# Gated attention's values turned through DRAM and VectorE instead of on TensorE

## The chip, the cores and the metric

The kernel runs on one core of a Trainium2 chip. The metric is the time of one execution on the device in microseconds (us); of the kernel before there are three runs, and their median counts.

The engines of the core work side by side, each through its own queue in order: TensorE (PE; PEld is its weight load), VectorE (DVE), ScalarE (ACT), GpSimd (POOL) and SyncE (SP). They wait for each other by semaphores. Matmuls write to PSUM, which has banks; the other data lie in SBUF, and weights and inputs in DRAM.

## What is computed

The reference is one block of a decoder: an RMS norm, one wide projection, two kinds of attention side by side (a forgetting attention with 8 heads and a gated linear attention with 4), their gated sum, an output projection, and a squared-ReLU MLP. There are 256 tokens and 16 learned meta tokens, 272 in all, and a model width of 2048. Cut to the gated attention:

```python
GLA_HEADS, GLA_DK, GLA_DV, GLA_CHUNK = 4, 256, 512, 64
def gated_linear_attention(q, k, v, g):
    # S_t = diag(alpha_t) S_{t-1} + k_t^T v_t,  o_t = q_t S_t, chunked
    ...
    q_dec, k_inv = qc * jnp.exp(b), kc * jnp.exp(-b)
    a = jnp.where(causal, einsum(q_dec, k_inv), 0.0)
    o_intra = einsum(a, vc)
    ...
o_gla = gated_linear_attention(gq, gk, gv, g_log)
o_gla = head_rmsnorm(o_gla, gla_norm_g) * silu(gr)
```

All is in float32.

## The kernel before

**Tiling.** Activations lie transposed: 128 features on the partitions, tokens along a row. Every projection is a gemm of one weight chunk (2048 x 128) with 16 steps of 128 features. To reach float32 accuracy, numbers are split in a high and a low part, and a step takes two matmuls (`gemm2`, lines 144 and 145, 512 and 256 columns) or three (`gemm_all`, lines 161 to 163, 272 columns). A weight chunk comes in two halves: SyncE's DMA fills `raw`, ScalarE casts the high part (line 128), VectorE subtracts it to get the low part (line 129), and the pair lies in one of five `wt` buffers. Gemm results come to one of three PSUM banks (pool `pg`); all other PSUM tiles share five (pool `px`).

**A head of gated attention** (`gla_head`) takes two key gemms, two query gemms, four value gemms (called V0 to V3 here) and four gate gemms. Each value gemm yields 128 of the head's 512 value columns, transposed: columns on the partitions, tokens along the row. Its eviction on VectorE scales it into `vT` (256 tokens, line 563) and `vE` (the last 16, line 564). The attention needs the values with tokens on the partitions, so `turn` transposes them: TensorE makes eight 128x128 transposes (lines 553 and 554) and one of 64x128 (line 555) as matmuls with the identity; ScalarE and VectorE split the first part to `v0`, and ScalarE copies the others to `v1` and `v2`.

`scores` multiplies queries and keys into the bank `pa` (line 535). ScalarE copies it (lines 536 and 537), GpSimd masks it with `affine_select` (line 542), and ScalarE and VectorE split it into `a0h` and `a0l` (lines 177 and 178). `outputs` multiplies scores and values into two `po` banks, copies them to `oT` and squares them to `so`. `sums` adds the squares over the partitions and takes the inverse root on VectorE (`root`, lines 206 to 212, whose room is `so`). `scale` multiplies `oT` by the norm's gain `ggn` and that factor (line 596), then by the gate `sg` (line 598), and splits the result to `og`.

**The order of the work.** `later(n, fn)` puts `fn` aside, and it runs when `n` further gemms have been issued; so `scores`, `turn`, `outputs`, `sums` and `scale` of one head are laid between the gemms of that head and the next. On each engine a list scheduler then fixes a queue. The attention's tiles lie in the pool `att` with one buffer for a tag, and `vT` and `so` have the same tag: the next head's values may only be written when the factor in `so` has been used.

Of the kernel before, what the change touches and what calls it, by code (L numbers as in the profile page):

```python
# [7 lines left out]
F32 = mybir.dt.float32  # L8
# [4 lines left out]
ALU = mybir.AluOpType  # L13
# [3 lines left out]
P = 128  # L17
D = 2048
KT = D // P
NM = 16  # L20
NT = 256
NA = NM + NT
EPS = 1e-6
FOX_H, FOX_D = 8, 128
GLA_H, GLA_DK, GLA_DV = 4, 256, 512
# [8 lines left out]
BIG = 3.0e38  # L34
RAW = 5
NL = 4

O_FQ, O_FK, O_FV, O_FF = 0, 1024, 2048, 3072
O_GQ, O_GK, O_GV, O_GR = 3080, 4104, 5128, 7176
# [29 lines left out]
def trunk(ctx: ExitStack, tc: tile.TileContext, hT, w_small, w_all, consts, w_alpha2, out):  # L69
    nc = tc.nc  # L70
    serial = [0]

    def nm(s):
        serial[0] += 1
        return f"{s}_{serial[0]}"
# [5 lines left out]
    dram = ctx.enter_context(tc.tile_pool(name="dram", bufs=1, space=bass.MemoryType.DRAM))  # L81
    pg = ctx.enter_context(tc.tile_pool(name="pg", bufs=3, space=PSUM))
    px = ctx.enter_context(tc.tile_pool(name="px", bufs=5, space=PSUM))
# [3 lines left out]
    def bank(pool, s):  # L87
        return pool.tile([P, 512], F32, tag="bank", name=nm(s))
# [5 lines left out]
    def later(n, fn):  # L94
        waiting.append([n, fn])
# [60 lines left out]
    def gemm_all(w, x, n=NA):  # L156
# [7 lines left out]
        issued()  # L164
        return ps

    def total(ps, t=None):

        b = tmp.tile([P, NT], F32, tag="evb", name=nm("evb"))
        nc.scalar.copy(b, ps[:, NT:512])  # L170
        if t is None:
            t = tmp.tile([P, NT], F32, tag="evt", name=nm("evt"), bufs=4)
        nc.vector.tensor_tensor(t, ps[:, 0:NT], b, op=ALU.add)  # L173
        return t

    def split_to(dst_hi, dst_lo, src):
        nc.scalar.copy(dst_hi, src)
        nc.vector.tensor_tensor(dst_lo, src, dst_hi.bitcast(F32), op=ALU.subtract)

    def split(pool, tag, src, bufs=None):  # L180

        kw = {} if bufs is None else {"bufs": bufs}
        hi = pool.tile(list(src.shape), F32R, tag=tag + "h", name=nm(tag + "h"), **kw)
        lo = pool.tile(list(src.shape), F32R, tag=tag + "l", name=nm(tag + "l"), **kw)
        split_to(hi, lo, src)
        return hi, lo
# [66 lines left out]
    ident, scan = cons[:, 0:P], cons[:, P : P + NA]  # L253
    ggn, ba, bf = cons[:, 400:416], cons[:, 416:424], cons[:, 424:425]
# [252 lines left out]
    def gla_head(hd, sg, ready=None):  # L507

        ki = att.tile([P, 2, NA], F32, tag="ki", name=nm("ki"))
        q0 = ready[0] if ready else att.tile([P, 2, NT], F32, tag="qd", name=nm("qd"))  # L510
        q1 = att.tile([P, 2, NT - G1], F32, tag="q1", name=nm("q1"))
        q2 = att.tile([P, 2, NM], F32, tag="q2", name=nm("q2"))
        k2 = att.tile([P, 2, 4, NM], F32, tag="k2", name=nm("k2"))
        for i in range(2):
            ps = ready[1] if ready and i == 0 else gemm_all(next_weights(), x)
            nc.vector.tensor_tensor(ki[:, i, :], ps[:, 0:NA], rb, op=ALU.mult)
        for i in range(2):
            t = q0[:, i, :] if ready else total(gemm2(next_weights(), xt))
            nc.vector.scalar_tensor_tensor(q0[:, i, :], t, GLA_DK ** -0.5, rbt, op0=ALU.mult, op1=ALU.mult)
        e = decay[hd]  # L520
        nc.vector.tensor_tensor(ki, ki, e[:, :, Q:], op=ALU.mult)
        nc.vector.tensor_copy(k2, ki[:, :, 2 * P :].unsqueeze(2).to_broadcast([P, 2, 4, NM]))
        nc.vector.tensor_tensor(q1, q0[:, :, G1:], e[:, :, NT : Q - NM], op=ALU.mult)
        nc.vector.tensor_tensor(q2, q0[:, :, G2:], e[:, :, Q - NM : Q], op=ALU.mult)
        nc.vector.tensor_tensor(q0, q0, e[:, :, 0:NT], op=ALU.mult)

        at1 = att.tile([P, NT - G1], F32, tag="at1", name=nm("at1"))

        def scores():
            pa = bank(px, "pa")  # L530
            p0, p1, p2 = pa[:, 0:NT], pa[:, NT : 2 * NT - G1], pa[0 : 4 * NM, 2 * NT - G1 : Q]
            for dst, k, q in ((p0, ki[:, :, 0:P], q0), (p1, ki[:, :, P : 2 * P], q1),
                              (p2, k2.rearrange("p a j s -> p a (j s)"), q2)):
                for a in range(2):
                    nc.tensor.matmul(dst, k[:, a, :], q[:, a, :], start=(a == 0), stop=(a == 1))  # L535
            nc.scalar.copy(at0, p0)
            nc.scalar.copy(at1, p1)
            nc.vector.tensor_tensor(at2[0 : 4 * NM].rearrange("p (j q) -> p j q", q=NM),
                                    p2.unsqueeze(1).to_broadcast([4 * NM, 4, NM]),
                                    diag[0 : 4 * NM].rearrange("p (j q) -> p j q", q=NM), op=ALU.mult)  # L540
            for ap, n, base in ((at0[:, 0:G1], G1, NM), (at1[:, 0:P], P, 0)):
                nc.gpsimd.affine_select(ap, ap, pattern=[[1, n]], compare_op=ALU.is_ge, fill=0.0, base=base,
                                        channel_multiplier=-1)

        v1 = att.tile([P, GLA_DV], F32, tag="v1", name=nm("v1"))
        vT = att.tile([P, 4, 2 * P], F32, tag="vT", name=nm("vT"))
        vE = att.tile([P, 4 * NM], F32, tag="vE", name=nm("vE"))

        def turn():
            pv = [bank(px, n) for n in ("p0", "p1", "p2")]  # L550
            for i in range(4):
                cols = slice(P * i, P * (i + 1))
                nc.tensor.transpose(pv[0][:, cols], vT[:, i, 0:P], ident)  # L553
                nc.tensor.transpose(pv[1][:, cols], vT[:, i, P : 2 * P], ident)
            nc.tensor.transpose(pv[2][0 : 4 * NM, 0:P], vE, ident)
            split_to(*v0, pv[0])
            nc.scalar.copy(v1, pv[1])
            nc.scalar.copy(v2[0 : 4 * NM], pv[2][0 : 4 * NM, 0:P])

        later(5, scores)  # L560
        for i in range(4):
            ps = gemm_all(next_weights(), x)
            nc.vector.tensor_tensor(vT[:, i, :], ps[:, 0 : 2 * P], rb[:, 0 : 2 * P], op=ALU.mult)
            nc.vector.tensor_tensor(vE[:, NM * i : NM * (i + 1)], ps[:, 2 * P : NA], rb[:, 2 * P :], op=ALU.mult)
        later(1, turn)

        oT = att.tile([P, 4, NT], F32, tag="oT", name=nm("oT"))
        st = {}

        def outputs():  # L570
            a0 = split(att, "a0", at0)
            so = st["so"] = att.tile([P, 4, NT], F32, tag="vT", name=nm("so"))
            po = [bank(px, "po").rearrange("p (j t) -> p j t", t=NT) for _ in range(2)]
            for c in range(4):
                three(po[c // 2][:, c % 2, :], [e[:, P * c : P * (c + 1)] for e in v0], a0, c % 2 == 0, False)
            for i, pj in enumerate(po):
                for j in range(2):
                    v = slice(P * (2 * i + j), P * (2 * i + j + 1))
                    nc.tensor.matmul(pj[:, j, G1:], v1[:, v], at1, start=False, stop=False)  # L579
                nc.tensor.matmul(pj[:, :, G2:], v2, at2[:, 2 * NM * i : 2 * NM * (i + 1)], start=False, stop=True)  # L580
                nc.scalar.copy(oT[:, 2 * i : 2 * i + 2, :], pj)
                nc.scalar.activation(so[:, 2 * i : 2 * i + 2, :], pj, AF.Square)
            nc.gpsimd.tensor_tensor(so[:, 0:2, :], so[:, 0:2, :], so[:, 2:4, :], op=ALU.add)
            nc.gpsimd.tensor_tensor(so[:, 0, :], so[:, 0, :], so[:, 1, :], op=ALU.add)
            st["sq"] = split(att, "sq", so[:, 0, :])

        def sums():
            pr = bank(px, "pr")[:, 0:NT]
            for i in range(2):
                nc.tensor.matmul(pr, ones_r, st["sq"][i], start=(i == 0), stop=(i == 1))  # L590
            st["y"] = root(pr, NT, 1.0 / GLA_DV, [st["so"][:, i, :] for i in (1, 2, 3, 3)])

        def scale():
            for i in range(4):
                j = 4 * hd + i
                nc.vector.scalar_tensor_tensor(oT[:, i, :], oT[:, i, :], ggn[:, j : j + 1], st["y"], op0=ALU.mult,
                                               op1=ALU.mult)
                nc.vector.tensor_tensor(oT[:, i, :], oT[:, i, :], st["sg"][:, i, :], op=ALU.mult)
                split_to(og_tile()[j][:, 0, :], og_tile()[j][:, 1, :], oT[:, i, :])

        later(2, outputs)
        later(3, sums)
        if sg is None:
            sg = gla_gates(None)
            st["sg"] = sg
            scale()
        else:
            st["sg"] = sg
            later(8, scale)

    att = cum.enter_context(tc.tile_pool(name="att", bufs=1, reuse_waits="tile"))

# [386 lines left out]
```

## Time and profile before

| | |
|---|---|
| median of 3 runs | 1596.85 us (1596.45 to 1598.58) |
| the profiled execution | 1599.16 us, of which the span is 1597.5 us |
| PE busy | 1587.4 us (99% of the span) |
| PEld busy | 1439.0 us (90%) |
| DVE busy | 1056.2 us (66%) |
| ACT busy | 780.0 us (49%) |
| POOL busy | 90.4 us (6%) |

The span runs from the first to the last recorded instruction; the execution's own time lies 1.7 us over it. A busy share is that of an engine's recorded instructions in the span. In a timeline each row has the start, the duration, the engine, the line of the kernel and what it writes and reads; "x4" says that four like instructions are drawn together. Durations of matmuls overlap, so the distance between two starts is what one takes of TensorE's time.

### The profile page before, as it was taken

What the parts mean: (1) busy time and instruction counts of PE and PEld (TensorE: products, weight loads), DVE (VectorE), ACT (ScalarE), POOL (GpSimd) and SP (SyncE); (2) the same over time, 40 slices, a digit from 0 to 9 for tenths busy, and PEclk for the clock granted to TensorE, in tenths of its full rate; (3) what the DMA queues carried; (4) which work ended last, traced back from release to release, by engine and by line L of the source; (5) the groups of instructions that cost most, each with busy time, mean ns of one, the idle gap of its engine ahead of it and who ended that gap; (6) DMA issues with size and microseconds to landing.
All of it is one profiled execution on the core that took longest, in us unless ns stands there. A gap on an engine that the chain in (4) does not pass through costs nothing.

```text
span 1597.5 us, 25251 instructions
## 1 busy us (share of the span) xinstructions
PE 1587.4 (99%) x9838; PEld 1439.0 (90%) x9838; DVE 1056.2 (66%) x1616; ACT 780.0 (49%) x1174; POOL 90.4 (6%) x139
## 2 busy tenths in 40 slices
PE   9999999999999999999999999999999999999998
PEld 8999999999998888888888888888888888888887
DVE  7777757575556656656677776667655776567665
ACT  6676444454445444444554443344433444344553
POOL 0000000010100000000012000000000000000011
PEclk9999999999999999999999999999999999999999
DMA  9444545455445555555565555555555555555552
GB/s 309 170 144 168 179 154 182 159 186 166 166 159 175 193 188 193 188 186 193 178 204 189 185 187 195 187 192 188 185 197 186 193 188 190 193 186 193 188 183 95
DMA packets 89464, 293.15 MB, mean 184 GB/s; under 512 B 9392, under 2 KB 19520, under 8 KB 89344
## 3 DMA queue, kind: packets, MB, share of 16 engines
q1 hardware_dynamic: 88176, 289.67, 54.0%
q0 software_dynamic: 448, 1.13, 0.3%
q8 instruction: 77, 1.26, 0.3%
q10 hardware_dynamic: 720, 0.74, 0.2%
q14 instruction: 43, 0.35, 0.1%
HBM read 289.39 MB, written 2.11 MB: 182 GB/s over the span
## 4 chain that ended last, share of the span: by engine, by line
PE 99%; DVE 0%; DMA 0%; ACT 0%; issue 0%; DVEq 0%; ACTq 0%
PE ps L144 50%; PE ps L145 27%; PE psa L162 5%; PE psa L161 5%; PE psa L163 5%; PE ps L359 1%; PE ps L892 1%; PE ps L366 1%; PE ps L879 0%; PE pa L535 0%; PE po L579 0%; PE psa L621 0%; DMA h<-hT_dram 0%; DVE scaled L924 0%; PE pq L691 0%; PE p L553 0%
## 5 line engine op out<-in xcount | busy, mean ns | idle before, releaser
L129 DVE TENSOR_TENSOR wt<-raw,wt 128x1024 fp32r<-128x1024 f32 x522 | 644.1, 1234 | 349.6 <-ACT wt L128 343.9
L128 ACT CAST wt<-raw 128x1024 fp32r<-128x1024 f32 x522 | 548.7, 1052 | 511.0 <-PE ps L145 277.5
L144 PE MATMUL ps<-x,wt 128*128 128x512 f32 x1952 | 679.8, 391 | 0.0
L145 PE MATMUL ps<-x,wt 128*128 128x256 f32 x1952 | 550.6, 282 | 0.0
L144 PEld LDWEIGHTS ps<-x,wt 128*128 128x128 f32 x1952 | 366.4, 188 | 75.8
L145 PEld LDWEIGHTS ps<-x,wt 128*128 128x128 f32 x1952 | 368.9, 189 | 0.2
L144 PE MATMUL ps<-a,wt 128*128 128x512 f32 x960 | 333.0, 390 | 0.0
L145 PE MATMUL ps<-a,wt 128*128 128x256 f32 x960 | 270.7, 282 | 0.0
L144 PEld LDWEIGHTS ps<-a,wt 128*128 128x128 f32 x960 | 180.1, 188 | 37.8
L145 PEld LDWEIGHTS ps<-a,wt 128*128 128x128 f32 x960 | 181.4, 189 | 0.0
L161 PE MATMUL psa<-x,wt 128*128 128x272 f32 x624 | 180.8, 290 | 0.0
L163 PE MATMUL psa<-x,wt 128*128 128x272 f32 x624 | 180.6, 289 | 0.0
L162 PE MATMUL psa<-x,wt 128*128 128x272 f32 x624 | 180.2, 289 | 0.0
L170 ACT COPY evb<-ps 128x256 f32<-128x256 f32 x160 | 59.4, 373 | 231.2 <-PE ps L145 229.3
L173 DVE TENSOR_TENSOR evt<-ps,evb 128x256 f32<-128x256 f32 x158 | 67.0, 425 | 100.0 <-ACT evb L170 99.8
L161 PEld LDWEIGHTS psa<-x,wt 128*128 128x128 f32 x624 | 117.2, 188 | 0.7
L162 PEld LDWEIGHTS psa<-x,wt 128*128 128x128 f32 x624 | 117.3, 188 | 0.0
L163 PEld LDWEIGHTS psa<-x,wt 128*128 128x128 f32 x624 | 117.2, 188 | 0.0
L144 PE MATMUL ps<-og,wt 128*128 128x512 f32 x256 | 89.2, 390 | 0.0
L144 PE MATMUL ps<-y,wt 128*128 128x512 f32 x256 | 88.8, 390 | 0.0
L802 POOL TENSOR_TENSOR acc<-acc,hsq 128x256 f32<-128x256 f32 x26 | 29.0, 1115 | 767.3 <-ACT hsq L801 767.3
L145 PE MATMUL ps<-og,wt 128*128 128x256 f32 x256 | 72.2, 282 | 0.0
(282 smaller groups left out, 1365.3 us busy)
## 6 DMA issues: line engine op xcount, KB each, us to landing
raw<-w_all_dram SPq DMA_DIRECT2D x536, 512.0 KB, 3.6
raw<-w_all_dram SPq DMA_DIRECT2D x6, 384.0 KB, 5.6
h<-hT_dram SPq DMA_DIRECT2D x6, 275.0 KB, 6.0
out_dram<-scaled SPq DMA_DIRECT2D x5, 256.0 KB, 2.7
negc<-fdram POOLq DMA_DIRECT2D x8, 136.0 KB, 3.9
raw<-w_all_dram SPq DMA_DIRECT2D x4, 256.0 KB, 5.2
raw<-w_all_dram SPq DMA_DIRECT2D x4, 192.0 KB, 5.1
room<-w_small_dram SPq DMA_DIRECT2D x1, 320.0 KB, 4.9
```

Source lines behind the costliest of these rows:

```text
L128: nc.scalar.copy(hi[:, k, :], r)
L129: nc.vector.tensor_tensor(lo[:, k, :], r, hi[:, k, :].bitcast(F32), op=ALU.subtract)
L144: nc.tensor.matmul(ps, hi, x, start=first, stop=False)
L145: nc.tensor.matmul(ps[:, 0:NT], lo, x[:, 0, :], start=False, stop=last)
L161: nc.tensor.matmul(ps[:, 0:n], hi, x[:, k, 0, :], start=(k == 0), stop=False)
L162: nc.tensor.matmul(ps[:, 0:n], lo, x[:, k, 0, :], start=False, stop=False)
L163: nc.tensor.matmul(ps[:, 0:n], hi, x[:, k, 1, :], start=False, stop=(k == KT - 1))
L170: nc.scalar.copy(b, ps[:, NT:512])
L173: nc.vector.tensor_tensor(t, ps[:, 0:NT], b, op=ALU.add)
L359: nc.tensor.matmul(ps, hi, x[:, k, :, NM:NA], start=st, stop=False)
L366: nc.tensor.matmul(ps[:, 0:NT], lo, x[:, k, 0, NM:NA], start=False, stop=sp)
L802: nc.gpsimd.tensor_tensor(acc, acc, sq, op=ALU.add)
```

## The change

The transposes leave TensorE. The value tile `vT` is laid out in blocks of 32 tokens. After the fourth value gemm, `move` (new) queues DMAs on GpSimd: `vT` and `vE` are written to DRAM (`rows` and `ends`) and read back so that 32x32 blocks have changed places between partitions and rows (four loads to `moved`, two to `last`). `turn` then is nine block transposes on VectorE, each of which turns every 32x32 block in its place. It is no longer a callback of its own; `outputs` calls it, queued on VectorE behind the latest gemm's eviction (`evicted`). `outputs` comes one gemm later than before, `sums` too. The product with `ggn` and the norm's factor moves from `scale` to the end of `sums`, and `scale` comes one gemm earlier. Cut to these parts:

```diff
@@ -164,13 +165,15 @@
+    evicted = [None]
+
     def total(ps, t=None):
...
-        nc.vector.tensor_tensor(t, ps[:, 0:NT], b, op=ALU.add)
+        evicted[0] = nc.vector.tensor_tensor(t, ps[:, 0:NT], b, op=ALU.add)
...
@@ -543,31 +547,43 @@
                                         channel_multiplier=-1)
 
         v1 = att.tile([P, GLA_DV], F32, tag="v1", name=nm("v1"))
-        vT = att.tile([P, 4, 2 * P], F32, tag="vT", name=nm("vT"))
+        vT = att.tile([P, 8, 4, SQ], F32, tag="vT", name=nm("vT"))
         vE = att.tile([P, 4 * NM], F32, tag="vE", name=nm("vE"))
 
+        def move():
+            rows = dram.tile([2 * P, 4 * P], F32, tag="rows", name=nm("rows"), bufs=2)
+            ends = dram.tile([P, 4 * NM], F32, tag="ends", name=nm("ends"), bufs=2)
+            nc.gpsimd.dma_start(rows.rearrange("(g p) e -> p g e", p=P), vT.rearrange("p (g j) c s -> p g (j c s)", j=4))
+            nc.gpsimd.dma_start(ends, vE)
+            moved = st["moved"] = att.tile([P, 2, 4, 4, SQ], F32, tag="oT", name=nm("moved"))
+            src = rows.rearrange("(b d) (j e) -> j d b e", d=SQ, e=P)
+            for j in range(4):
+                nc.gpsimd.dma_start(moved[SQ * j : SQ * (j + 1)].rearrange("p g i c s -> p (g i) (c s)"), src[j])
+            moved = st["last"] = att.tile([P, 4, SQ], F32, tag="k2", name=nm("last"))[0 : 2 * SQ]
+            src = ends.rearrange("(b d) (j e) -> j d b e", d=SQ, e=SQ)
+            for j in range(2):
+                nc.gpsimd.dma_start(moved[SQ * j : SQ * (j + 1)], src[j])
+
         def turn():
-            pv = [bank(px, n) for n in ("p0", "p1", "p2")]
-            for i in range(4):
-                cols = slice(P * i, P * (i + 1))
-                nc.tensor.transpose(pv[0][:, cols], vT[:, i, 0:P], ident)
-                nc.tensor.transpose(pv[1][:, cols], vT[:, i, P : 2 * P], ident)
-            nc.tensor.transpose(pv[2][0 : 4 * NM, 0:P], vE, ident)
-            split_to(*v0, pv[0])
-            nc.scalar.copy(v1, pv[1])
-            nc.scalar.copy(v2[0 : 4 * NM], pv[2][0 : 4 * NM, 0:P])
+            turned = att.tile([P, GLA_DV], F32, tag="vT", name=nm("turned"))
+            for g, dst in ((0, turned), (1, v1)):
+                for c in range(4):
+                    nc.vector.transpose(dst[:, P * c : P * (c + 1)], st["moved"][:, g, :, c, :])
+            nc.vector.transpose(v2[0 : 4 * NM], st["last"].rearrange("p i s -> p (i s)"))
+            split_to(*v0, turned)
 
         later(5, scores)
         for i in range(4):
             ps = gemm_all(next_weights(), x)
-            nc.vector.tensor_tensor(vT[:, i, :], ps[:, 0 : 2 * P], rb[:, 0 : 2 * P], op=ALU.mult)
+            nc.vector.tensor_tensor(vT[:, :, i, :], ps[:, 0 : 2 * P].rearrange("p (j s) -> p j s", s=SQ),
+                                    rb[:, 0 : 2 * P].rearrange("p (j s) -> p j s", s=SQ), op=ALU.mult)
             nc.vector.tensor_tensor(vE[:, NM * i : NM * (i + 1)], ps[:, 2 * P : NA], rb[:, 2 * P :], op=ALU.mult)
-        later(1, turn)
-
-        oT = att.tile([P, 4, NT], F32, tag="oT", name=nm("oT"))
-        st = {}
+        move()
 
         def outputs():
+            with tc.issue_after(evicted[0].ins):
+                turn()
+            oT = st["oT"] = att.tile([P, 4, NT], F32, tag="oT", name=nm("oT"))
             a0 = split(att, "a0", at0)
             so = st["so"] = att.tile([P, 4, NT], F32, tag="vT", name=nm("so"))
             po = [bank(px, "po").rearrange("p (j t) -> p j t", t=NT) for _ in range(2)]
@@ -588,25 +604,28 @@
             pr = bank(px, "pr")[:, 0:NT]
             for i in range(2):
                 nc.tensor.matmul(pr, ones_r, st["sq"][i], start=(i == 0), stop=(i == 1))
-            st["y"] = root(pr, NT, 1.0 / GLA_DV, [st["so"][:, i, :] for i in (1, 2, 3, 3)])
-
-        def scale():
+            y = root(pr, NT, 1.0 / GLA_DV, [st["so"][:, i, :] for i in (1, 2, 3, 3)])
             for i in range(4):
                 j = 4 * hd + i
-                nc.vector.scalar_tensor_tensor(oT[:, i, :], oT[:, i, :], ggn[:, j : j + 1], st["y"], op0=ALU.mult,
+                nc.vector.scalar_tensor_tensor(st["oT"][:, i, :], st["oT"][:, i, :], ggn[:, j : j + 1], y, op0=ALU.mult,
                                                op1=ALU.mult)
+
+        def scale():
+            oT = st["oT"]
+            for i in range(4):
+                j = 4 * hd + i
                 nc.vector.tensor_tensor(oT[:, i, :], oT[:, i, :], st["sg"][:, i, :], op=ALU.mult)
                 split_to(og_tile()[j][:, 0, :], og_tile()[j][:, 1, :], oT[:, i, :])
 
-        later(2, outputs)
-        later(3, sums)
+        later(3, outputs)
+        later(4, sums)
         if sg is None:
             sg = gla_gates(None)
             st["sg"] = sg
             scale()
         else:
             st["sg"] = sg
-            later(8, scale)
+            later(7, scale)
 
     att = cum.enter_context(tc.tile_pool(name="att", bufs=1, reuse_waits="tile"))
 
```

What this does to the order of instructions shows at three places. In the rows, names carry running numbers; a row is line, operation, output, inputs and size, and `x4` says how many alike follow each other.

The first is TensorE at head 0's scores and turn (`p_115` to `p_117` are the transposed values, `psa_1113` and `psa_1108` a value gemm). Before:

```order
L535 MATMUL pa_1074<-qd_543,ki_625 128x256 x2
L535 MATMUL pa_1074<-q_63_626,ki_625 128x144 x2
L535 MATMUL pa_1074<-q_64_627,k_65_628 64x16 x2
L553 MATMUL p_115_1086<-cons,vT_733 128x128
L554 MATMUL p_116_1087<-cons,vT_733 128x128
...
L554 MATMUL p_116_1087<-cons,vT_733 128x128
L555 MATMUL p_117_1088<-cons,vE_734 64x128
L163 MATMUL psa_1113<-x,wt_1109 128x272
```

Now:

```order
L163 MATMUL psa_1108<-x,wt_1104 128x272
L539 MATMUL pa_1085<-qd_543,ki_625 128x256 x2
L539 MATMUL pa_1085<-q_63_626,ki_625 128x144 x2
L539 MATMUL pa_1085<-q_64_627,k_65_628 64x16 x2
L164 MATMUL psa_1108<-x,wt_1104 128x272
L162 MATMUL psa_1108<-x,wt_1104 128x272
```

The gemm goes on right behind the scores; no transposes stand between.

The second is VectorE from the end of head 0's factor to the eviction of head 1's V0 (`so` holds the factor, `psa_1358` and `psa_1370` are V0). Before:

```order
L212 SCALAR_TENSOR_TENSOR so_1196<-so_1196 128x256
L596 SCALAR_TENSOR_TENSOR oT_1009<-oT_1009,cons,so_1196 128x256 x4
L598 TENSOR_TENSOR oT_1009<-oT_1009,sg_611 128x256
L129 TENSOR_TENSOR wt_1655<-raw_1654,wt_1655 128x8x128
L598 TENSOR_TENSOR oT_1009<-oT_1009,sg_611 128x256 x2
L563 TENSOR_TENSOR vT_1346<-psa_1358,rb 128x256
L564 TENSOR_TENSOR vE_1347<-psa_1358,rb 128x16
L563 TENSOR_TENSOR vT_1346<-psa_1449,rb 128x256
L564 TENSOR_TENSOR vE_1347<-psa_1449,rb 128x16
```

Now, where `pa_1711` are head 1's scores and `a0l_1837` is the low part of them:

```order
L130 TENSOR_TENSOR wt_1731<-raw_1730,wt_1731 128x8x128
L214 SCALAR_TENSOR_TENSOR so_1248<-so_1248 128x256
L542 TENSOR_TENSOR at_513<-pa_1711,corners 64x64
L181 TENSOR_TENSOR a0l_1837<-at_512,a0h_1836 128x256
L215 SCALAR_TENSOR_TENSOR so_1248<-so_1248 128x256
L610 SCALAR_TENSOR_TENSOR oT_1243<-oT_1243,cons,so_1248 128x256 x4
L617 TENSOR_TENSOR oT_1243<-oT_1243,sg_611 128x256 x3
L578 TENSOR_TENSOR vT_1358<-psa_1370,rb 128x8x32
L580 TENSOR_TENSOR vE_1359<-psa_1370,rb 128x16
L578 TENSOR_TENSOR vT_1358<-psa_1461,rb 128x8x32
```

The two rows of head 1's scores (lines 542 and 181) now come ahead of the last root step, of the product with `ggn` and of V0's eviction; before, they came after the evictions of V0, V1 and V2.

The third is TensorE at the start of head 1's last value gemm V3 (`psa_1579`, `psa_1604`), with the engines that a row waits for. Before:

```order
L163 MATMUL psa_1518<-x,wt_1514 128x272
L535 MATMUL pa_1692<-qd_1011,ki_1010 128x256 x2
L535 MATMUL pa_1692<-q_106_1012,ki_1010 128x144 x2
L535 MATMUL pa_1692<-q_107_1013,k_108_1014 64x16 x2
L553 MATMUL p_186_1704<-cons,vT_1346 128x128 [waits DVE_49]
L554 MATMUL p_187_1705<-cons,vT_1346 128x128
L161 MATMUL psa_1579<-x,wt_1570 128x272 [waits DVE_49,Activation_49]
```

Now (`pa_1711` are the scores, `psa_1530` is V2):

```order
L164 MATMUL psa_1530<-x,wt_1526 128x272
L539 MATMUL pa_1711<-qd_1022,ki_1021 128x256 [waits DVE_49]
L539 MATMUL pa_1711<-qd_1022,ki_1021 128x256
L539 MATMUL pa_1711<-q_109_1023,ki_1021 128x144 x2
L539 MATMUL pa_1711<-q_110_1024,k_111_1025 64x16 x2
L162 MATMUL psa_1604<-x,wt_1595 128x272 [waits DVE_49,Activation_49]
```

V3's first matmul waits for VectorE and ScalarE as before; the two transposes ahead of it, and their wait, are gone.

## Rows read from the trace of the kernel before

**Rows 1.** The page: busy time, share of the span and instructions of each engine
```profile
PE 1587.4 (99%) x9838; PEld 1439.0 (90%) x9838; DVE 1056.2 (66%) x1616; ACT 780.0 (49%) x1174; POOL 90.4 (6%) x139
```

**Rows 2.** TensorE's waits, whole run: line, releaser, us in total, times, longest
```profile
PE warm L330 <- DVE cons L252: 1.3, 1, 1.3
PE pn L912 <- ACT sq L897: 0.8, 1, 0.8
PE ps L359 <- DVE x L347: 0.8, 1, 0.8
PE pn L919 <- DVE ry L817: 0.3, 1, 0.3
```

**Rows 3.** The timeline of TensorE: start, us, engine, line, operation
```profile
95.17 0.33 PE L553 MATMUL p<-cons,vT 128*128 128x128 f32 x1
...
96.13 0.37 PE L163 MATMUL psa<-x,wt 128*128 128x272 f32 x1
...
133.51 0.33 PE L553 MATMUL p<-cons,vT 128*128 128x128 f32 x1
...
133.70 0.37 PE L161 MATMUL psa<-x,wt 128*128 128x272 f32 x1
...
145.06 0.39 PE L144 MATMUL ps<-x,wt 128*128 128x512 f32 x1
...
145.40 0.27 PE L553 MATMUL p<-cons,vT 128*128 128x128 f32 x1
...
146.09 0.48 PE L144 MATMUL ps<-x,wt 128*128 128x512 f32 x1
...
295.69 0.33 PE L553 MATMUL p<-cons,vT 128*128 128x128 f32 x1
...
296.64 0.48 PE L144 MATMUL ps<-x,wt 128*128 128x512 f32 x1
```

**Rows 4.** VectorE's instructions of line 522 (min/median/max duration in ns)
```profile
L522 DVE COPY k<-ki x4: 220/222/225, 88.4 to 259.2; 128x128 f32<-128x128 f32 x4
```

**Rows 5.** The timeline of VectorE between the heads 0 and 1
```profile
129.30 1.68 DVE L596 SCALAR_TENSOR_TENSOR oT<-oT,cons,so 128x256 f32<-128x256 f32 x4
130.89 0.42 DVE L598 TENSOR_TENSOR oT<-oT,sg 128x256 f32<-128x256 f32 x1
...
132.36 0.75 DVE L598 TENSOR_TENSOR oT<-oT,sg 128x256 f32<-128x256 f32 x2
133.03 0.42 DVE L563 TENSOR_TENSOR vT<-psa,rb 128x256 f32<-128x256 f32 x1
133.37 0.17 DVE L564 TENSOR_TENSOR vE<-psa,rb 128x16 f32<-128x16 f32 x1
```

**Rows 6.** DMA issues of the page, and GpSimd's timeline with two of them
```profile
negc<-fdram POOLq DMA_DIRECT2D x8, 136.0 KB, 3.9
...
329.84 1.15 POOL L657 DMA_DIRECT2D negc<-fdram  x2 [20.64 <-DVE oT L598]
```

**Rows 7.** The timeline of ScalarE and VectorE, head 0's scores
```profile
96.03 0.41 ACT L177 CAST a0h<-at 128x256 fp32r<-128x256 f32 x1 [0.20 <-POOL at L542]
...
96.47 0.43 DVE L178 TENSOR_TENSOR a0l<-at,a0h 128x256 fp32r<-128x256 f32 x1 [0.36 <-ACT a0h L177]
```

**Rows 8.** The timeline of VectorE, head 3's factor
```profile
324.93 0.42 DVE L212 SCALAR_TENSOR_TENSOR so<-so 128x256 f32<-128x256 f32 x1
325.39 1.67 DVE L596 SCALAR_TENSOR_TENSOR oT<-oT,cons,so 128x256 f32<-128x256 f32 x4
```

**Rows 9.** TensorE's timeline at the start; slices of the end (PEclk: granted clock)
```profile
6.30 2.90 PE L359 MATMUL ps<-x,wt 128*128 128x512 f32 x6 [0.81 <-DVE x L347]
...
10.89 1.55 PE L359 MATMUL ps<-x,wt 128*128 128x512 f32 x6
...
1590.50:1591.00 0.50, 0.12 (x2) 0.00 (x0) 0.34 (x2) 0.00 (x0) 0.00 (x0) 1.00 0.00 0
...
1591.50:1592.00 0.50, 0.00 (x0) 0.00 (x0) 0.50 (x2) 0.00 (x0) 0.00 (x0) 0.50 0.26 78
```

More of the change, by code (lines that the diff above doesn't have):

```diff
@@ L36 @@
 NL = 4
+SQ = 32
 O_FQ, O_FK, O_FV, O_FF = 0, 1024, 2048, 3072
@@ L515, in gla_head @@
             ps = ready[1] if ready and i == 0 else gemm_all(next_weights(), x)
-            nc.vector.tensor_tensor(ki[:, i, :], ps[:, 0:NA], rb, op=ALU.mult)
+            evicted[0] = nc.vector.tensor_tensor(ki[:, i, :], ps[:, 0:NA], rb, op=ALU.mult)
         for i in range(2):
@@ L525, in gla_head @@
         nc.vector.tensor_tensor(q0, q0, e[:, :, 0:NT], op=ALU.mult)
+        st = {}
         at1 = att.tile([P, NT - G1], F32, tag="at1", name=nm("at1"))
```

## The prediction

> **What bounds the kernel now.** I read the page first [rows 1]: TensorE is busy for 99% of the span and VectorE for 66%, so time is won by taking work from TensorE and lost by making it wait. Next I read TensorE's waits, four in the whole run [rows 2]: three at the first input load or the last norm, one (0.8 us) at the start. None lies between 60 and 330 us, where the gated attention runs. There, TensorE's own instructions set the time. Then I read the timelines where the change touches TensorE and VectorE; what follows rests on those and on the order of instructions shown above.
>
> The times shown have a median of 1596.85 us. The profiled execution took 1599.16 us, 2.31 us more; I sum against the latter and carry the difference over to the median. About 0.2%, or 3.2 us, is what a measurement can tell from no change.
>
> **What is removed.** Each head's 9 transposes stand on TensorE between matmuls that waited for nothing. From the first one's start to the start of the next other matmul: head 0, 95.17 to 96.13, 0.96 us; head 1, in two pieces, 133.51 to 133.70 and 145.40 to 146.09, 0.88; head 3, 295.69 to 296.64, 0.95 [rows 3]; head 2 is taken as head 3. The sum is 0.96 + 0.88 + 0.95 + 0.95 = **3.74 us**. That is 0.10 us per transpose, though each row shows 0.27 to 0.33 us, because matmuls overlap and only the distance of starts counts.
>
> The Trainium skill prices it otherwise: "VectorE: DVE Perf Modes", section The three transpose paths, has 390 ns for a 128x128 transpose on TensorE, by which 36 would return 14.0 us and the sum would end near 1590.1 us, an estimate from that page; its Rules for kernel authors advise TensorE where a PSUM destination will do, which speaks against the change. The trace doesn't bear the 390 ns out as a cost, since starts lie 0.11 us apart.
>
> Copies that ScalarE loses and the final `ggn` product's move between callbacks are counted at nothing by themselves, as no TensorE wait in the stretch hangs on them.
>
> **What is added off the path.** VectorE gets 9 block transposes per head. The trace has none, so I bound one: below by the 128x128 copy, 222 ns [rows 4]; above by the 128x256 product with a bank of PSUM, 0.42 us [rows 5]. I take 0.28, near the lower end because the elements agree. That is 2.5 us per head, 10 in all, on an engine that is idle for a third of the span: no cost while the weight halves stay ahead. If that cover went, it would be those 2.5 us per head.
>
> GpSimd's queue gets two stores and six loads per head. A comparable POOL transfer (136 KB) lands 3.9 us after its issue, and issuing one takes about 0.6 us (two in 1.15) [rows 6]. The store, four to six issues and a landing make 0.6 + 3.9 + 6 x 0.6 + 3.9 = 12.0 us at the outside; with issues under way while the store lands, about 10.5. The turned values are wanted only after three gate gemms, each of 16 steps of 0.34 us (145.06 to 145.40 [rows 3]): 16.3 us from V3's end, less some 0.8 for its eviction and 2.5 for the transposes, leaves 13.0. I count nothing for it, with a late round trip as a rival. GpSimd's `affine_select` of head 0 is queued behind those loads, which have landed well before that head's outputs need it.
>
> **What is moved, and the new wait.** The important place is head 1's last value gemm, V3. The gemm pool has three banks, so V3's first matmul waits until VectorE has evicted V0. Before, V0's two evictions ran at 133.03 and 133.37, ended at 133.54, and V3 started at 133.70 [rows 3, 5]: just in time, and without a wait. These evictions cannot come earlier, because `vT` shares one buffer with head 0's `so`, which holds the norm's factor until `scale` (now `sums`) has used it.
>
> In the changed order VectorE reaches the low half of head 1's scores (`a0l`) *ahead* of head 0's last root step, the four products with `ggn` and V0's evictions. VectorE takes its queue in order, so these all wait for `a0l`. That in turn needs TensorE's scores `pa`, ScalarE's copy, GpSimd's mask and ScalarE's cast. TensorE issues `pa` right before V3. So V3 waits for a chain that begins only when its predecessor has finished.
>
> The chain, from the moment at which V3 could have started:
> - To the start of `a0l`: 96.47 - 95.17 = 1.30 us, by the same steps in head 0 [rows 3, 7].
> - `a0l` holds VectorE for 0.34, the spacing of 128x256 products (133.03 to 133.37) [rows 5]: 1.64.
> - The last root step to the first dependent product: 325.39 - 324.93 = 0.46 [rows 8]: 2.10.
> - Four products: 130.89 - 129.30 = 1.59 [rows 5]: 3.69.
> - Three products with the gate, at (133.03 - 132.36) / 2 = 0.335 each [rows 5]: 4.69.
> - V0's evictions: 0.34 + 0.17, and about 0.1 for the signal: **5.3 us**.
>
> V3 would start near 132.6 + 5.3 = 137.9. Before the chain VectorE has, by my reading, some 0.4 us to spare, so the other side of the estimate is a wait of up to 6.2 us. The products, unlike the transposes, are shown in the trace; the wait hardly depends on the transposes' or the DMA's price. Behind V3's wait on TensorE stands everything; behind `a0l` on VectorE stand the evictions and the next weight halves, of which five buffers are filled ahead.
>
> **The clock.** After its last matmuls of the run (0.12 us of work left in the slice from 1590.50) the granted clock went from 1.00 to 0.50, that is 2.4 to 1.2 GHz, by the slice at 1591.50 [rows 9]. A stop of 5.3 us at V3 should therefore lower it. For the way back, at the kernel's start six 512-column matmuls took 2.90 us at 6.30 and 1.55 at 10.89 [rows 9]. Over the 4.4 us until the faster rate, (1 - 1.55 / 2.90) x 4.4 = 2.0 us were lost. Bounds: 0 if the clock holds; 4.4 if the slow stretch has to be counted from the first matmul at about 1.3 us (9.4 us long). I take **2.0**, the row after a short gap.
>
> **Sum.** -3.74 + 5.3 + 2.0 = +3.56 us: the profiled execution would be 1602.7, the median **1600.4**. Its own range is 1598.6 (0.2 us of clock) to 1603.7 (a wait of 6.2 and 4.4 of clock).
>
> **Rivals.**
> - *The wait comes, the clock holds.* For it: the column still read 1.00 in the slice that holds the run's last matmuls, although TensorE had waited twice shortly before [rows 2, 9]. Against it: those waits were 0.8 and 0.3 us, and this one is 5.3. +5.3 - 3.74 = +1.6: 1598.4.
> - *No wait at V3, faster.* It decides if V0's evictions get ahead of `a0l`, or if V3's semaphore asks for an earlier VectorE instruction than V0's eviction: then TensorE passes unhindered. The point is the eviction's end: if it comes within some 0.2 us of `pa`'s, as before, nothing is lost. For it: the order lists only which engine V3 waits for, as in the kernel before. Against it: three banks for three earlier gemms. Then -3.74: 1593.1.
> - *The round trip through DRAM is late as well.* It decides when the transposes' data land later than about 13 us after V3's eviction; I have 10.5 to 12.0. For it: eight queued transfers in place of none, beside the weight stream. Against it: bytes are few. With 3 us on one head 1603.4, with 3 us on each of heads 1 to 3 up to 1609.4. The Trainium skill, "SBUF — State Buffer", has a box on a "DVE blocks DMA" trap: descriptors of a DMA issued from GpSimd starve while VectorE runs certain two-port operations, and it compares about 620 ns with 3100. By that, an estimate, one such delay of 2.5 us would use up most of the slack and two would exceed it. No row here shows whether it happens.
> - *The block transposes are dear*, at 0.42 or more, and VectorE falls behind: 36 x 0.14 = 5 us of VectorE work, still mostly hidden; perhaps +1, 1601.4.
>
> That the change doesn't do what it says is excluded: the order shows the transposes gone.
>
> **Numbers.** Wait and slow clock 0.52, wait with the clock holding 0.18, no wait 0.10, late round trip 0.13, dear transposes 0.07. The range 1597.0 to 1604.0 takes in the first two with their bounds, a late round trip on one head and the dear transposes, and leaves out the fast case and late trips on several heads. Faster by over 0.2% (below 1593.65): 0.10. Within it (to 1600.05): the clock's case and some two fifths of the first, with a little of the others, 0.40. Slower: 0.50.
>
> **What would show it.** TensorE's waits in the new profile should hold one long entry, `psa` waiting for VectorE's `vE` or `vT` at head 1, of 5 to 6 us and once. The rows after it should show 512-column or 272-column matmuls at twice their spacing for some microseconds. The transposes should be near 0.28 us. I am wrong if that entry is missing or under 3 us, if further long waits stand at `po` (late transposes or loads) or at weights, or if the matmuls after the gap keep their pace.

## The result: slower by 0.24%, by a wait of 5.3 us and a lowered clock

The changed kernel takes 1600.47 us (median of 11 runs, 1599.67 to 1602.95), the kernel before 1596.94 us (11 runs, 1596.35 to 1598.58). The ratio is 1.0024 with a 95% interval of 1.0015 to 1.0033; the medians lie 3.53 us apart, where +3.56 was forecast.

The page of the changed kernel has nearly the same shares of busy time as [rows 1] (GpSimd one point more), with 3.7 us less on TensorE:

```profile
PE 1583.7 (99%) x9802; PEld 1435.6 (90%) x9802; DVE 1061.9 (66%) x1652; ACT 776.6 (49%) x1166; POOL 109.1 (7%) x171
```

TensorE's waits of the changed kernel, which answer to [rows 2] (line, what released it, us in total, times, longest):

```profile
PE psa L162 <- ACT og L180: 5.3, 1, 5.3
PE warm L333 <- DVE cons L255: 1.3, 1, 1.3
PE pn L931 <- ACT sq L916: 0.8, 1, 0.8
PE ps L362 <- DVE x L350: 0.4, 1, 0.4
PE pn L938 <- DVE ry L836: 0.3, 1, 0.3
```

One line is new, at the forecast place and of the forecast length. The timeline of VectorE in the changed kernel, answering to [rows 5], shows what ran before it:

```profile
131.11 0.49 DVE L214 SCALAR_TENSOR_TENSOR so<-so 128x256 f32<-128x256 f32 x1
131.52 0.21 DVE L542 TENSOR_TENSOR at<-pa,corners 64x64 f32<-64x64 f32 x1
131.80 0.42 DVE L181 TENSOR_TENSOR a0l<-at,a0h 128x256 fp32r<-128x256 f32 x1
132.14 0.42 DVE L215 SCALAR_TENSOR_TENSOR so<-so 128x256 f32<-128x256 f32 x1
132.59 1.67 DVE L610 SCALAR_TENSOR_TENSOR oT<-oT,cons,so 128x256 f32<-128x256 f32 x4
134.18 1.09 DVE L617 TENSOR_TENSOR oT<-oT,sg 128x256 f32<-128x256 f32 x3
135.19 0.42 DVE L578 TENSOR_TENSOR vT<-psa,rb 128x256 f32<-128x256 f32 x1
135.52 0.17 DVE L580 TENSOR_TENSOR vE<-psa,rb 128x16 f32<-128x16 f32 x1
```

And TensorE, around its wait:

```profile
130.13 0.41 PE L539 MATMUL pa<-q,k 128*64 128x16 f32 x4
135.83 0.56 PE L162 MATMUL psa<-x,wt 128*128 128x272 f32 x1 [5.30 <-ACT og L180]
136.19 0.43 PE L163 MATMUL psa<-x,wt 128*128 128x272 f32 x1
136.42 0.43 PE L164 MATMUL psa<-x,wt 128*128 128x272 f32 x1
...
139.37 0.35 PE L162 MATMUL psa<-x,wt 128*128 128x272 f32 x1
139.56 0.28 PE L163 MATMUL psa<-x,wt 128*128 128x272 f32 x1
139.68 0.29 PE L164 MATMUL psa<-x,wt 128*128 128x272 f32 x1
```

V0's eviction ends at 135.52 + 0.17 = 135.69, and V3 starts at 135.83. The profile names ScalarE's cast to `og` as what released it. That is a guess between two events that ended almost together: three such casts ran on ScalarE from 134.63 for 1.08 us, to 135.71. V3 needs nothing from `og`; of ScalarE it needs a weight cast, and the last one before the wait ran from 128.89 for 1.04 us. The run with four gemm banks, below, settles it.

Behind the wait the matmuls lie 0.23 us apart (136.19 to 136.42) until 139.37, and 0.12 after it. The slices of the changed kernel show the same in the granted clock, the column after POOL's:

```profile
130.00:132.00 2.00, 0.54 (x6) 0.31 (x4) 1.94 (x4) 0.96 (x3) 0.73 (x2) 1.00 0.50 156
132.00:134.00 2.00, 0.00 (x0) 0.00 (x0) 1.96 (x6) 0.00 (x0) 0.00 (x0) 0.67 0.64 211
134.00:136.00 2.00, 0.17 (x1) 0.20 (x2) 2.00 (x8) 1.08 (x3) 0.00 (x0) 0.50 0.14 57
136.00:138.00 2.00, 2.00 (x9) 2.00 (x10) 2.00 (x9) 0.41 (x1) 0.00 (x0) 0.50 0.00 0
138.00:140.00 2.00, 2.00 (x12) 2.00 (x12) 0.19 (x1) 0.00 (x0) 0.00 (x0) 0.63 0.00 0
140.00:142.00 2.00, 2.00 (x18) 2.00 (x17) 0.16 (x1) 1.05 (x1) 0.00 (x0) 1.00 0.00 0
```

The clock goes to 0.50 (1.2 GHz) while TensorE stands still, and stays there for the first microseconds of work.

The added work shows these prices in the changed kernel: its block transposes (minimum, median and maximum in ns), and its DMAs (KB each, us to landing):

```profile
L571 DVE STREAM_TRANSPOSE turned<-moved x16: 267/272/315, 98.0 to 305.9; 128x128 f32<-128x128 f32 x16
```

```profile
rows<-vT POOLq DMA_DIRECT2D x4, 512.0 KB, 4.2
moved<-rows POOLq DMA_DIRECT2D x16, 128.0 KB, 6.1
```

### The profile page after: what moved, and what is told of

Read it like the earlier page. It is cut to its first block, busy times and chain, and to the rows that moved or that the text cites. A ratio compares the mean times of both kernels' runs of the same rounds, so it can differ in the third digit from the quotient of the medians.

```text
span 1598.6 us, 25276 instructions
## 1 busy us (share of the span) xinstructions
PE 1583.7 (99%) x9802; PEld 1435.6 (90%) x9802; DVE 1061.9 (66%) x1652; ACT 776.6 (49%) x1166; POOL 109.1 (7%) x171
## 4 chain that ended last, share of the span: by engine, by line
PE 97%; issue 1%; DVE 1%; ACT 0%; DMA 0%; POOL 0%; DVEq 0%; ACTq 0%; POOLq 0%
PE ps L145 50%; PE ps L146 27%; PE psa L162 5%; PE psa L164 5%; PE psa L163 5%; PE ps L362 1%; PE ps L911 1%; PE ps L369 1%; PE ps L898 0%; PE pa L539 0%; PE psa L640 0%; PE po L595 0%; DMA h<-hT_dram 0%; DVE scaled L943 0%; PE pq L710 0%
```

## The experiments

Two theories were to be told apart. By the **prediction's** words, V3 waits because two operations on head 1's scores stand ahead of the evictions in VectorE's queue. The other: the **factor is late by itself**, wherever these stand, and V0 can't be evicted before it has been used, because `vT` and `so` share a buffer. Each run is timed beside the kernel before on the same chip.

### The root's room in other memory

```diff
-            pr = bank(px, "pr")[:, 0:NT]
+            both = bank(px, "pr")
+            pr = both[:, 0:NT]
...
-            y = root(pr, NT, 1.0 / GLA_DV, [st["so"][:, i, :] for i in (1, 2, 3, 3)])
+            y = root(pr, NT, 1.0 / GLA_DV, [both[:, NT : 2 * NT]] + [v1[:, NT * i : NT * (i + 1)] for i in (0, 1, 1)])
```

> The root's room leaves so: its first operand goes to the free half of the bank of the sums, the rest to v1, which is idle then. Head 1's values may then be evicted before head 0's factor is finished. Theory (V3 waits because V0's eviction waits for the factor in the shared buffer): no wait of TensorE between 60 and 330 us, so 5.3 us of wait and about 1.5 us of lowered clock go, 1600.5 - 6.8 = 1593.7 us. Rival (the DMAs or the block transposes hold VectorE or the banks up): the wait stays, over 3 us, and the time stays near 1600.

Measured: 1593.44 us against 1596.73, ratio 0.9979 (0.997 to 0.9988). TensorE's waits in this kernel:

```profile
PE warm L333 <- DVE cons L255: 1.3, 1, 1.3
PE pn L932 <- ACT sq L917: 0.8, 1, 0.8
PE ps L362 <- DVE x L350: 0.3, 1, 0.3
PE pn L939 <- DVE ry L837: 0.3, 1, 0.3
PE ps L912 <- DVE h L900: 0.2, 1, 0.2
```

No wait is left at V3. V0 is now evicted at 117.26 us, and the products with `ggn` run only at 133.83, when V3 is nearly over (it ends at 134.4): V3 no longer needs the factor. The scheduler also moved head 1's scores behind V3 here, so the run `a0l_behind` below has to tell what their place alone does. DMAs and block transposes are all there and cost nothing that can be seen; what's left is the gain from the removed transposes, 3.3 us. This version is faster than both kernels: by 3.3 us than the one before, and by 7.0 than the changed one (1600.47 - 1593.44).

### The same room in the kernel before

The same edit in the kernel before, where the root's result goes to `st["y"]`.

> The kernel before with only the root's room moved out of so, as in room_elsewhere. The kernel before has no wait at V3, so there is nothing to gain: 1596.7 us within 0.2%. If it falls to 1593.5, the gain of room_elsewhere is the room's and not the removed transposes'.

Measured: 1596.87 us against 1596.80, ratio 1.0000 (0.9992 to 1.0009). So the room by itself brings nothing, and the 3.3 us of the run above belong to the rest of the change, of which only the removed transposes take work from TensorE.

### Four banks for gemms

```diff
-    pg = ctx.enter_context(tc.tile_pool(name="pg", bufs=3, space=PSUM))
-    px = ctx.enter_context(tc.tile_pool(name="px", bufs=5, space=PSUM))
+    pg = ctx.enter_context(tc.tile_pool(name="pg", bufs=4, space=PSUM))
+    px = ctx.enter_context(tc.tile_pool(name="px", bufs=4, space=PSUM))
```

> The changed kernel with four banks for gemms and four for the rest in place of three and five. V3 then needs no bank of V0's; the first gate gemm does, 16 x 0.375 = 6 us later, when the eviction is over. Theory (V3 waits for V0's bank): no wait over 1 us at head 1, 1593.5 to 1595 us. Rival (V3 waits for something else on VectorE): the wait stays and the time stays near 1600. The pool with four banks may add short waits of its own.

Measured: 1593.83 us against 1596.80, ratio 0.9980 (0.9972 to 0.9989), and no wait of TensorE at head 1. Yet VectorE evicts V0 no earlier, as its timeline in this kernel shows:

```profile
131.81 1.67 DVE L610 SCALAR_TENSOR_TENSOR oT<-oT,cons,so 128x256 f32<-128x256 f32 x4
...
135.54 0.42 DVE L578 TENSOR_TENSOR vT<-psa,rb 128x256 f32<-128x256 f32 x1
```

With a fourth bank nobody waits for it: V3's last matmul starts at 134.26, before V0's eviction, and most of V3 runs before the first cast to `og` (133.89). So it is V0's bank that V3 waited for, not the casts that the profile names. The scheduler moved the scores behind V3 in this run too.

### The scores' operations behind the evictions

```diff
-            nc.vector.tensor_tensor(at2[0 : 4 * NM].rearrange("p (j q) -> p j q", q=NM),
+            with tc.issue_after(st["v2"].ins):
+              nc.vector.tensor_tensor(at2[0 : 4 * NM].rearrange("p (j q) -> p j q", q=NM),
...
-            a0 = split(att, "a0", at0)
+            with tc.issue_after(st["v2"].ins):
+                a0 = split(att, "a0", at0)
```

Here `st["v2"]` is V2's last eviction.

> Only VectorE's two operations on head 1's scores are queued behind V2's eviction; all else as in the changed kernel. If their place ahead of the evictions is the whole cause (as the prediction says it), the wait at V3 goes and the time falls to about 1594. If VectorE is late by itself, because the factor is begun one gemm later, only the time between the end of the last second-to-last root step and the last root step goes, 132.14 - 131.5 = 0.6 us: a wait of 4.7 us, 1599.9 us.

Measured: 1600.35 us against 1596.73, ratio 1.0023 (1.0014 to 1.0032). TensorE's wait and VectorE's timeline in this kernel:

```profile
PE psa L162 <- ACT og L180: 4.8, 1, 4.8
```

```profile
131.01 0.49 DVE L214 SCALAR_TENSOR_TENSOR so<-so 128x256 f32<-128x256 f32 x1
131.54 0.42 DVE L215 SCALAR_TENSOR_TENSOR so<-so 128x256 f32<-128x256 f32 x1
```

With nothing between the last two steps of the root, the wait falls by 0.5 us and the clock still falls (0.50 in the slices from 134 to 138 us). The median is only 0.1 us lower, within the noise of the two runs. So the scores' place was the last link of the chain, but a small part of its length: without it the root's own steps would have ended the wait almost as late.

### Only the counts, in the kernel before

```diff
-        later(2, outputs)
-        later(3, sums)
+        later(3, outputs)
+        later(4, sums)
```

> The kernel before, transposes on TensorE, with nothing changed but outputs and sums one gemm later (3 and 4 in place of 2 and 3). If the late factor is what makes V3 wait, a wait of 3 to 5 us appears at head 1 here too, with the lowered clock: 1597 + 3 to 5 + 1.5 = 1601.5 to 1603.5 us. If the way through DRAM and VectorE is the cause, or the place of the scores' operations, none appears and the time stays at 1597.

Measured: 1599.23 us against 1596.73, ratio 1.0018 (1.0010 to 1.0027). TensorE, V0's eviction on VectorE, and two slices of this kernel:

```profile
133.31 0.33 PE L553 MATMUL p<-cons,vT 128*128 128x128 f32 x1 [2.28 <-DVE vT L563]
```

```profile
132.83 0.42 DVE L563 TENSOR_TENSOR vT<-psa,rb 128x256 f32<-128x256 f32 x1
```

```profile
130.00:132.00 2.00, 1.03 (x9) 0.76 (x8) 2.00 (x4) 0.97 (x3) 0.49 (x1) 1.00 0.64 219
132.00:134.00 2.00, 0.69 (x6) 0.70 (x7) 2.00 (x9) 0.92 (x3) 1.30 (x2) 1.00 0.32 92
```

A wait appears with no DMA, no block transpose and the scores' operations behind the evictions: the later factor alone makes 2.3 us. It stands at the two transposes right ahead of V3, which read the evicted values. It was expected at 3 to 5 us, and in the profiled execution (1598.69 us) the clock didn't fall: its 2.0 us over the kernel before are no more than the wait. The 11 times lie in two groups, though: six from 1598.43 to 1599.23 us, among them the profiled one, and five from 1600.84 to 1602.10. The mean granted clock of the five is 0.997 or 0.998, that of the six 0.998 or 0.999; so the clock may have fallen in the five, but no trace of one was kept. The median's 2.5 us mixes the two groups.

### The old counts, in the changed kernel

The reverse edit: 2 and 3 in the changed kernel.

> The changed kernel with outputs and sums at the old counts (2 and 3). Theory (late factor): the wait at V3 falls under 1 us, but the turned values come too late now: in the changed kernel the low half of the values was ready 2.1 to 2.5 us before its first use, and the use moves 5.4 us forward, so TensorE waits about 3 us at the outputs of each of the four heads: 1600.5 - 6.8 + 12 = 1606 us, between 1600 and 1610. If there is slack enough, no wait at the outputs and 1594 us.

Measured: 1604.86 us against 1596.73, ratio 1.0044 (1.0030 to 1.0057); the five times spread from 1600.75 to 1606.98. TensorE's waits in the profiled execution (1605.10):

```profile
PE psa L162 <- ACT og L180: 4.8, 1, 4.8
PE po L193 <- ACT a0h L180: 3.7, 2, 2.6
```

Half of it came as expected: outputs now wait, though at two places with 3.7 us in all, not at four with 12. The other half did not: V3's wait stays at 4.8. The counts put the root's first step at 118.49, only 1.5 us earlier than in the changed kernel (119.97), and VectorE put other work between: a weight half of 1.30 us at 132.44 comes ahead of V0's eviction. The waits are 3.2 us longer in sum than the changed kernel's, the profiled execution 4.8 us: the second wait for the outputs, 2.6 us at head 3 up to 309.58, also lowered the granted clock, to 0.50 in this slice:

```profile
310.00:312.00 2.00, 2.00 (x8) 1.80 (x8) 2.00 (x6) 1.69 (x2) 0.00 (x0) 0.50 0.16 57
```

Counts are no cure, in either direction.

### Without the way through DRAM

```diff
-            turned = att.tile([P, GLA_DV], F32, tag="vT", name=nm("turned"))
+            turned = att.tile([P, GLA_DV], F32, tag="oT", name=nm("turned"))
...
-                    nc.vector.transpose(dst[:, P * c : P * (c + 1)], st["moved"][:, g, :, c, :])
-            nc.vector.transpose(v2[0 : 4 * NM], st["last"].rearrange("p i s -> p (i s)"))
+                    nc.vector.transpose(dst[:, P * c : P * (c + 1)], vT[:, 4 * g : 4 * g + 4, c, :])
+            nc.vector.transpose(v2[0 : 4 * NM], vT[0 : 4 * NM, 0:4, 0, :])
...
-        move()
```

> The changed kernel without the DMAs of the values: the block transposes read the value tile in SBUF itself. This leaves out the exchange of the blocks between partitions, so the attention's values are others; every other instruction stays. If the way through DRAM, when it runs, makes head 0's outputs and so the factor late, the wait at V3 shrinks by 2 us or more, to about 3 us, and the time to 1597 or 1598. If what counts is the place that outputs and the root's steps have in the queues, which hardly changes here, the wait stays between 4 and 5.5 us and the time between 1599 and 1600.5.

Measured: 1599.65 us against 1596.89, ratio 1.0017 (1.0008 to 1.0027). TensorE's wait:

```profile
PE psa L162 <- ACT og L180: 4.3, 1, 4.3
```

It stays, 1.0 us shorter, between the bounds of the second case. TensorE doesn't wait for the turned values in the changed kernel either, so it is mainly the place of `outputs` and of the root's steps in the queues that counts. The 1.0 us are an upper bound for the transfers: the scheduler gave VectorE another order in this run (`a0l`, at 132.61, comes behind the products with `ggn`, at 130.84).

### TensorE kept busy in the wait

```diff
+            if hd == 1:
+                idle = bank(px, "idle")[:, 0:NT]
+                for i in range(9):
+                    nc.tensor.matmul(idle, ki[:, 0, 0:P], q0[:, 0, :], start=True, stop=True)
             nc.scalar.copy(at0, p0)
```

> The changed kernel with nine more matmuls of 256 columns in float32 behind head 1's scores, whose result nobody reads: about 3.9 us of work inside the wait at V3. Theory (the wait lowers the clock and that costs 1.5 us by itself): the rest of the wait is about 1.4 us, the matmuls behind it come 0.125 us apart as elsewhere, and the time is 1600.4 - 1.5 = 1598.9 us, while V3 starts at the same point. Rival (V3's slow matmuls have another cause, or the clock falls in the rest all the same): spacing 0.23 us and 1600.4 us.

Measured: 1599.03 us against 1596.80, ratio 1.0015 (1.0007 to 1.0024). TensorE in this kernel:

```profile
130.73 4.15 PE L543 MATMUL idle<-qd,ki 128*128 128x256 f32 x18
136.09 0.36 PE L162 MATMUL psa<-x,wt 128*128 128x272 f32 x1 [1.21 <-ACT og L180]
136.29 0.29 PE L163 MATMUL psa<-x,wt 128*128 128x272 f32 x1
136.42 0.29 PE L164 MATMUL psa<-x,wt 128*128 128x272 f32 x1
```

V3 still starts about 5.4 us after `pa`, but its matmuls come 0.13 us apart at once. Work that nobody needs makes the kernel 1600.47 - 1599.03 = 1.4 us faster (1.3 by the two distances from the kernel before, 3.53 and 2.23). That is the clock's share alone.

### The factor's product at once, in the kernel before

```diff
             st["y"] = root(pr, NT, 1.0 / GLA_DV, [st["so"][:, i, :] for i in (1, 2, 3, 3)])
-
-        def scale():
             for i in range(4):
                 j = 4 * hd + i
                 nc.vector.scalar_tensor_tensor(oT[:, i, :], oT[:, i, :], ggn[:, j : j + 1], st["y"], op0=ALU.mult,
                                                op1=ALU.mult)
+
+        def scale():
+            for i in range(4):
+                j = 4 * hd + i
...
-            later(8, scale)
+            later(7, scale)
```

> The kernel before with only the product of ggn and the factor moved to sums, and scale one gemm earlier (7). All theories that put the loss on the late factor say no change: 1596.7 us within 0.2%, and no new wait of TensorE. If that part of the change loses or wins by itself, over 1 us shows here.

Measured: 1596.51 us against 1596.80, ratio 0.9998 (0.9989 to 1.0007). This part of the change neither costs nor gains anything clear of the noise, and TensorE has no new wait.

## Why the prediction was right, and where its reasons were not

**The sum** held: +3.56 us forecast, +3.53 measured, the range held it, and slower had the highest chance.

**The removed transposes**, 3.74 us by the distance of starts: 3.3 us in `room_elsewhere`, where they are gone and nothing waits. Right, and a little high. The sentence on the Trainium skill's price has its answer too: at the 390 ns that the page gives for one in bf16 ("VectorE: DVE Perf Modes", The three transpose paths), an estimate of 14.0 us would have come back. Here they cost 3.3 us / 36 = 0.09 us each. Its advice to transpose on TensorE is borne out by the changed kernel as it stands, and not by the version with the room elsewhere, which gains by moving them.

**The wait at V3**: 5.3 us forecast, 5.30 measured, step by step as told (only the releaser that the profile names, `og`, is not the one foretold). `a0l` starts at 131.80, 1.27 us after V3 could have started (135.83 - 5.30 = 130.53), where 1.30 was taken [rows 3, 7]; the products start at 132.59 (2.06 against 2.10), and the evictions at 135.19 (4.66 against 4.69). Between the root step ahead of it (131.11 + 0.34) and `a0l` (131.80) VectorE had 0.35 us, where 0.4 were told; 0.2 of them went to the scores' other operation, line 542. The bound of 6.2 us for the wait is worked out nowhere: 5.3 and 0.4 don't make it.

**What failed is the reason given for its length**: "V3 waits for a chain that begins only when its predecessor has finished". The chain is there, but it hides a second that ended nearly as late: take the scores' operations out of it, and 4.8 us remain. The prediction counted the time after `a0l` and didn't ask when the factor would have come without it. In the kernel before, the products began at 129.30 [rows 5], over 4 us ahead of V3's start at 133.70 [rows 3]; in the changed kernel they begin at 132.59, 2.1 us after V3 could have started.

What makes the 5.3 us, by the runs: later counts, 2.3 (`before_late`). There TensorE could go on at 133.31 - 2.28 = 131.03 and V0's eviction began at 132.83, 1.8 us later; in the changed kernel 4.66 us lie between, 2.9 more. To see which engine moved, count both traces from the start of head 0's scores, in `before_late` and in the changed kernel:

```profile
90.87 1.03 PE L535 MATMUL pa<-qd,ki 128*128 128x256 f32 x4
```

```profile
91.17 1.03 PE L539 MATMUL pa<-qd,ki 128*128 128x256 f32 x4
```

TensorE could go on 131.03 - 90.87 = 40.16 us behind them there, and 130.53 - 91.17 = 39.36 here: 0.8 of the 2.9 us are its earlier arrival, close to what head 0's transposes had taken, 0.96 [rows 3]. V0's eviction began 41.96 us behind them there and 44.02 here: 2.1 us are VectorE's delay. Of those, the scores' place accounts for 0.5 (`a0l_behind`) and the way through DRAM for up to 1.0 (`no_trip`). The remaining 0.6 us or more go with the other order that the scheduler made, which no run took apart; the delay is there before the factor is begun, as the root's first step starts 2.7 us later by this count (119.97 - 91.17 against 116.97 - 90.87). The gain itself brings TensorE sooner to a wait: that is part of why it was given back.

**The clock**: 2.0 us forecast from [rows 9], 1.4 by `keep_busy`. In the trace, fifteen matmuls of V3 took 139.37 - 135.83 = 3.54 us; at 0.125 us each they take 1.9, so 1.6 were lost. The mechanism was right and the term 0.4 to 0.6 too large; the transposes' term, 0.4 too large the other way, cancelled it. That the sum came within 0.03 us is luck. The rival with the clock holding falls for this wait. For the wait of 2.3 us in the profiled execution of `before_late` the granted clock stayed 1.00.

**The profiled execution** of the kernel before lay 2.3 us above the median. Most of that now has a reason: its first gemms ran at the slow rate [rows 9], in the changed kernel's execution they hardly did:

```profile
5.92 1.84 PE L362 MATMUL ps<-x,wt 128*128 128x512 f32 x6 [0.43 <-DVE x L350]
...
8.67 1.56 PE L362 MATMUL ps<-x,wt 128*128 128x512 f32 x6
```

From the first row's start to the second's are 2.75 us here and 4.59 in [rows 9], 1.8 us less. So the two profiles differ by 1.1 us (1600.28 and 1599.16) and the medians by 3.5; carrying the difference over to the median was right, and the 1602.7 us told for the profiled execution itself were 2.4 too many.

**The way through DRAM** was under-priced and harmless. Head 3 in the changed kernel, from the store's issue to the first use of the low half of the turned values:

```profile
291.35 0.72 POOL L556 DMA_DIRECT2D rows<-vT  x1 [47.02 <-DVE vE L580]
```

```profile
305.32 0.89 DVE L571 STREAM_TRANSPOSE turned<-moved 128x128 f32<-128x128 f32 x4 [0.88 <-DMA moved<-rows]
308.54 0.68 DVE L181 TENSOR_TENSOR v0l<-turned,v0h 128x512 fp32r<-128x512 f32 x1
```

```profile
311.74 0.28 PE L195 MATMUL po<-a0h,v0l 128*128 128x256 f32 x1
```

The trip takes 14.0 us (291.35 to 305.32), where 10.5 to 12.0 were taken and 13.0 called the limit. Loads land 6.1 us after their issue, not 3.9 as [rows 6] suggested. VectorE stood idle for it, TensorE did not: the low half is ready at 309.22 and first used at 311.74, so 2.5 us were to spare. The limit was too strict: the first outputs start at 309.30, 18.0 us after the store's issue, and use only the high half. With `counts_early` the rival of late values came true in part. The box that the Trainium skill has in "SBUF — State Buffer" on DMAs starved by VectorE can't be judged from this: no run here separates it from the loads' own time.

**Block transposes**: 0.28 us forecast, 0.272 measured. They weren't dear.

## What to carry to other kernels

Taking work from the busiest engine pays only if what that engine meets next is ready sooner as well; ask of every buffer with one copy when its last reader is done, before and after the change. A chain that explains a wait to the digit is not yet its cause: take its links away one at a time, and count the chain that ends next. Here the cure was three kilobytes per partition that lay idle at that time, or one more bank, not another order of the work.

## What was not expected of the hardware

Stops of 5.3, 4.8 and 4.3 us at V3 took the granted clock to 0.50, and so did one of 2.6 us (`counts_early`, head 3); one of 2.3 us (`before_late`) left it at 1.00 in both slices around it, in the one execution that was traced. These runs give no length of a stop that is safe. Filling the stop down to 1.2 us with useless matmuls kept it at full rate and made the kernel 1.4 us faster.
